# First two heads' scores moved into the projection's tail: one stretch of program order in place of two

## The chip, the cores and the metric

The kernel runs on one core of one Trainium2 chip. The metric is the device time of one execution in microseconds, as the median of several runs. Five engines work side by side, each in the order of its own queue: TensorE (PE, with its weight loads as PEld), VectorE (DVE), ScalarE (ACT), GpSimd (POOL) and SyncE (SP), which issues the transfers.

## The reference

One layer of a diffusion trunk over 1024 latent tokens and 128 context tokens, width 1024. Both token sets are normalised and modulated, then projected once. Group A is a gated MLP that mixes positions inside chunks of 128. Group B is attention with four heads, low-rank queries and keys, and a rotary part of 64. The two are gated, joined and projected out. The part that matters here is attention:

```python
def _block_attention(q_nope, q_ropes, key_sets):
    ...
        for qr, (kn, kr, _) in zip(q_ropes, key_sets):
            logits.append(jnp.einsum('bqhn,bkhn->bhqk', qn, kn)
                          + jnp.einsum('bqhr,bkr->bhqk', qrb, kr))
        s = jnp.concatenate(logits, axis=-1).astype(jnp.float32) * ATTN_SCALE
        p = jax.nn.softmax(s, axis=-1).astype(v_all.dtype)
        return jnp.einsum('bhqk,bkhv->bqhv', p, v_all)
```

Latent tokens read all 1024 latent keys and 256 cached context keys in one softmax. The 128 context tokens of the new request read only themselves. All inputs and outputs are fp32.

## The kernel before

The tokens are nine tiles of 128 (0 to 7 latent, 8 context), in three groups of three tiles. Every fp32 product is made of three (or five) products in a reduced fp32 format: each operand is split into a rounded part and a remainder (names ending in h and l), the rounded part by a cast on ScalarE or GpSimd, the remainder by `lo_of`, a subtraction on VectorE.

The program has these parts: loading, modulating and the v columns; the twelve channel blocks of the wide projection (`channels`); the narrow projection z (448 columns: query rank 256, key rank 128, rope 64), tile by tile in `z_chunk`, with the work that follows from each tile woven between; attention; the output projection.

The weaving is written out by hand. `run((cost, fn))` emits one TensorE step and moves a model clock by its cost; `later(dt, fn)` puts work of the other engines on a list, to be emitted when the model clock has passed its time; `merged` mixes two lists of steps; `need` emits waiting work until a result is marked as made. Inside a block of `tc.manual_schedule` the instructions of PE, ACT, DVE and POOL stay in the order in which they are emitted. An engine's queue is in order, so an instruction that waits holds all behind it.

After the last z tile (t = 8), the projection's tail holds: key transposes (`keys`, kT), the transpose of the last query latents (`cq_transpose(8)`), rotary queries of tiles 6 to 8 (`q_rope`, `q_rope_T`: tiles qr and qrT), and the unrotated queries of group 2 for four heads (`q_nope(2, h)`: qn20 to qn23). The norm of each tile is in `z_stats`: z is copied, squared and summed, and `scales` and `apply` give kvn, scl and nscl. These steps use eight PSUM banks: `pst` (tag t, two banks given out in turn) and `psa` (tag acc, six banks given out in turn). Behind them this block ends, all its pending work is emitted, `psa` is closed, and attention opens `pso` (tag o, one bank) and `pss` (two score tiles s1 of two banks each and one bank s2 for the context part) in its place. A tile that takes an older tile's bank waits until that one has been read.

Attention works through 32 pairs of tile and head. `score_steps(t, h)` gives two latent halves of five 512-wide products (s) and a context part of five 256-wide ones (s2). `softmax` then does, on VectorE, two row maxima (m) and the shift nb; on ScalarE the exponentials (e) with their sums; on VectorE the reciprocal (rs); on GpSimd the scaling of e. Scores run two heads (LEAD) ahead. `value_steps` transposes the probabilities of a pair of heads (pT in `pst`), splits them (ph, pl), multiplies with the values (o) and up-projects (at). `own_steps` is the context tile's attention with itself: scores s8, transposes pT8, product o8 and up-projection at8.

## Time and profile before

| | |
|---|---|
| median of 3 runs | 630.7 us (629.14 to 634.01) |
| the profiled execution | 633.54 us, its span 631.5 us |
| mean granted clock of TensorE | 0.993 |
| busy in the span | PE 97%, PEld 88%, DVE 57%, ACT 42%, POOL 28% |
| chain that ended last | PE 90%, DVE 3%, DMA 3%, ACT 3% |
| z projection, last block starts | 315.2 us |
| projection's tail | 315.4 to 326.8 us |
| first head's scores start | 326.8 us |
| last matmul starts | 623.8 us |

Times inside the execution are counted from the start of the span. The profile's engine rows give the start, the length and the tiles of each instruction, and in brackets how long the engine stood idle before it and which engine ended that. Matmuls overlap, so the distance between two starts says what a matmul costs, and its length is more than that.

### The profile page before, as it was taken

Reading aid. Unit: us, or ns where it says so; the run is one execution under the profiler, and the core shown is the slowest. Engines: PE = TensorE matmul, PEld = TensorE weight load, DVE = VectorE, ACT = ScalarE, POOL = GpSimd, SP = SyncE. Lnnn points to the kernel's source line nnn. Section 1 sums busy time; section 2 is a strip of 40 time slices with the busy share of each in tenths; the row PEclk is TensorE's granted clock in tenths of the full one; section 3 lists DMA queues with packets and bytes.
Section 4 is the critical chain, followed back from the end, with each engine's and each line's share of the span. In section 5 each row is a group of like instructions: output and inputs, shape, how many; then the busy total and the mean of one; then the engine's idle time right before and its main releaser. Section 6 shows DMA issues by size and latency. Waiting matters only on the chain.

```text
span 631.5 us, 9855 instructions
## 1 busy us (share of the span) xinstructions
PE 615.5 (97%) x3733; PEld 558.3 (88%) x3733; DVE 359.0 (57%) x835; ACT 264.2 (42%) x635; POOL 175.2 (28%) x217
## 2 busy tenths in 40 slices
PE   7999999999999999999989999999999999999995
PEld 6677889999999999999977999999999988888884
DVE  2667347037766200356786665776766755487655
ACT  7444774012111011465566556555555543132212
POOL 2525104154433520243353221332222341000001
PEclk8999999999999999999999999999999999999999
DMA  8975100024122430100010000000101112523311
GB/s 324 370 277 169 34 0 2 1 72 178 52 84 95 126 119 1 32 7 1 0 42 2 1 1 0 2 2 34 34 1 34 34 68 84 184 100 134 107 60 66
DMA packets 17118, 46.32 MB, mean 73 GB/s; under 512 B 1952, under 2 KB 6448, under 8 KB 17072
## 3 DMA queue, kind: packets, MB, share of 16 engines
q1 hardware_dynamic: 16928, 45.51, 20.9%
q8 instruction: 29, 0.48, 0.3%
q10 hardware_dynamic: 144, 0.20, 0.1%
q14 instruction: 17, 0.14, 0.1%
HBM read 40.87 MB, written 4.83 MB: 72 GB/s over the span
## 4 chain that ended last, share of the span: by engine, by line
PE 90%; DVE 3%; DMA 3%; ACT 3%; SPq 1%; issue 1%; ACTq 0%
PE tp L670 6%; PE tp L151 6%; PE tp L150 6%; PE tp L152 6%; PE pT L1142 5%; PE w L1389 5%; PE w L1390 5%; PE w L1391 5%; PE o L1166 3%; PE o L1168 3%; PE o L1167 3%; PE s L1097 3%; PE s L1098 3%; PE s L1096 3%; PE s L1095 3%; PE s L1099 3%
## 5 line engine op out<-in xcount | busy, mean ns | idle before, releaser
L104 DVE TENSOR_TENSOR pl<-pT,ph 128x512 fp32r<-128x512 f32 x81 | 55.4, 686 | 48.0 <-ACT ph L1146 47.9
L1086 POOL TENSOR_SCALAR e<-e,rs 128x1280 f32<-128x1280 f32 x32 | 42.8, 1338 | 137.1 <-DVE rs L1085 121.4
L152 PE MATMUL tp<-area,w2l 128*128 128x384 f32 x216 | 72.5, 336 | 0.0
L150 PE MATMUL tp<-area,w2h 128*128 128x384 f32 x216 | 72.5, 336 | 0.0
L151 PE MATMUL tp<-area,w2h 128*128 128x384 f32 x216 | 72.5, 336 | 0.0
L1080 ACT ACTIVATE e<-s,nb,scl 128x256 f32<-128x256 f32 x64 | 56.1, 881 | 36.0 <-DVE nb L1074 35.9
L1146 ACT CAST ph<-pT 128x512 fp32r<-128x512 f32 x80 | 45.4, 589 | 43.2 <-PE pT L1142 40.2
L1142 PE MATMUL pT<-ident,e 128*128 128x128 f32 x320 | 47.9, 272 | 0.6 <-DVE pl L104 0.6
L1166 PE MATMUL o<-ph,vh 128*128 128x256 f32 x160 | 47.8, 299 | 0.0
L104 DVE TENSOR_TENSOR w2l<-w2r,w2h 128x1024 fp32r<-128x1024 f32 x12 | 20.2, 1687 | 43.9 <-POOL w2h L107 43.9
L1168 PE MATMUL o<-ph,vl 128*128 128x256 f32 x160 | 44.9, 281 | 0.0
L1167 PE MATMUL o<-pl,vh 128*128 128x256 f32 x160 | 44.7, 280 | 0.0
L1391 PE MATMUL w<-area,ml 128*128 128x512 f32 (+1 forms) x114 | 43.2, 379 | 0.0
L1142 PEld LDWEIGHTS pT<-ident,e 128*128 128x128 f32 x320 | 37.5, 140 | 4.3 <-DVE pl L104 1.5
L150 PEld LDWEIGHTS tp<-area,w2h 128*128 128x128 f32 x216 | 40.5, 188 | 0.6 <-issue 0.5
L151 PEld LDWEIGHTS tp<-area,w2h 128*128 128x128 f32 x216 | 40.5, 188 | 0.2
L152 PEld LDWEIGHTS tp<-area,w2l 128*128 128x128 f32 x216 | 40.5, 188 | 0.0
L1070 DVE TENSOR_REDUCE m<-s 128x1 f32<-128x1024 f32 x32 | 38.9, 1216 | 1.9 <-PE s L1099 1.9
L1095 PE MATMUL s<-kch,area 128*128 128x512 f32 (+2 forms) x100 | 38.9, 389 | 0.0
L670 PE MATMUL tp<-area,w2h 128*128 128x384 f32 x144 | 37.4, 340 | 0.0
L1098 PE MATMUL s<-krh,area 128*128 128x512 f32 (+2 forms) x100 | 35.4, 354 | 0.0
L1097 PE MATMUL s<-kch,area 128*128 128x512 f32 (+2 forms) x100 | 35.4, 354 | 0.0
(309 smaller groups left out, 1583.6 us busy)
## 6 DMA issues: line engine op xcount, KB each, us to landing
ada<-in_ada_ss SPq DMA_DIRECT2D x16, 512.0 KB, 10.9
w2r<-in_w_t SPq DMA_DIRECT2D x12, 512.0 KB, 4.1
xr<-in_x SPq DMA_DIRECT2D x9, 512.0 KB, 5.0
adag<-in_ada_g SPq DMA_DIRECT2D x8, 512.0 KB
wor<-in_w_o SPq DMA_DIRECT2D x8, 512.0 KB, 3.2
out_y<-y SPq DMA_DIRECT2D x8, 512.0 KB, 2.7
x<-in_x SPq DMA_DIRECT2D x6, 512.0 KB, 8.7
wvr<-in_w_v SPq DMA_DIRECT2D x8, 256.0 KB, 8.2
```

The costliest lines, as they stand in the source:

```text
L104: V.tensor_tensor(lo, src, f32(hi), op=ALU.subtract)
L150: T.matmul(ps, wh, xh, start=j == 0, stop=False)
L151: T.matmul(ps, wh, xl, start=False, stop=False)
L152: T.matmul(ps, wl, xh, start=False, stop=j == n - 1)
L670: T.matmul(tps[i, g][:, :GW], w_[i][:, k, :], x_[k, g], start=k == 0 and j == 0, stop=k == NK - 1 and j == 2)
L1080: S.activation(e[:, sl], src, AF.Exp, bias=nb, scale=scl[:, t : t + 1], accum_out=su[:, i : i + 1])
L1095: T.matmul(ps, qh_, kch[:, sl], start=True, stop=False)
L1142: T.transpose(ps[:, w : w + P], es[t, h][:, c * P : (c + 1) * P], ident)
L1166: T.matmul(o, vh[:, kt, :], ph[:, sl], start=c == 0, stop=False)
L1167: T.matmul(o, vh[:, kt, :], pl[:, sl], start=False, stop=False)
L1168: T.matmul(o, vl[:, kt, :], ph[:, sl], start=False, stop=c == n - 1)
L1391: T.matmul(ps, b, woh[k][:, c0:c1], start=False, stop=k == NK - 1)
```

## The change

Projection and attention become one block of program order. `psa` is closed right behind `cq_transpose(8)`, and `pso` and `pss` are opened there. The scores of the first two heads (tile 0, heads 0 and 1), which stood behind the tail, stand among its steps. The tail's own tiles therefore no longer have `psa`: rotary queries of tiles 6 to 8 and unrotated queries of heads 0 and 2 take `pst`, those of heads 1 and 3 take the one bank of `pso`, and the last tile's keys share one `pst` tile at the end (`keys_last`). The query latents cq are kept per group, those of groups 0 and 1 in an own pool that is closed early, and the probabilities of the first two heads get an own pool (e0).

Of the other engines' work: the last tile's squares and norm are due later, the exponentials' table is loaded 2.6 model units behind the key transposes and not at the end, the values' copies on GpSimd are due earlier, and in `scales` the two VectorE operations zv are emitted together in a step of their own. The context tile's own attention moves back: its scores from the first two heads to the next two, its other steps by one round, and o8 takes a `pst` bank.

```diff
@@ z_stats
-                V.tensor_scalar(v[:, c_], ssz[:, c_], 1.0 / width, EPS, op0=ALU.mult, op1=ALU.add)
+            def mean():
+                V.tensor_scalar(v[:, 0:1], ssz[:, 0:1], 1.0 / 256.0, EPS, op0=ALU.mult, op1=ALU.add)
+                V.tensor_scalar(v[:, 1:2], ssz[:, 1:2], 1.0 / 128.0, EPS, op0=ALU.mult, op1=ALU.add)
...
+            at_ = 4.5 if t == NT - 1 else 0.35
             for i, op in enumerate(steps_):
-                later(0.35 + 0.2 * i, op)
-            later(0.35 + 0.2 * len(steps_), lambda: apply(r))
+                later(at_ + 0.2 * i, op)
+            later(at_ + 0.2 * len(steps_), lambda: apply(r))
...
-        later(0.35, squares)
+        last = t == NT - 1
+        later(2.6 if last else 0.35, squares)
         later(0.9, rope_key)
-        later(1.5, scales)
+        later(4.0 if last else 1.5, scales)
@@ q_nope, q_rope, q_rope_T
-        ps = psa.tile([P, 512], F32, tag="acc", name=f"qn{g}{h}")
+        pool = psa if g < 2 else (pst, pso)[h % 2]
+        ps = pool.tile([P, 512], F32, tag="acc" if g < 2 else "to"[h % 2], name=f"qn{g}{h}")
...
-        ps = psa.tile([P, 512], F32, tag="acc", name=f"qr{t}")
+        ps = (pst if t == NS else psa).tile([P, 512], F32, tag="t" if t == NS else "acc", name=f"qr{t}")
...
-        late = t == NS
+        late = t >= 6
@@ new
+    def keys_last():
+        need(("k", NS))
+        ps = pst.tile([P, 512], F32, tag="t", name="kT8")
+        T.transpose(ps[:, 0:P], kvn[:, NS, :], ident)
+        T.transpose(ps[:, P : 2 * P], krd[:, NS, :, :].rearrange("p a r -> p (a r)"), ident)
+        sl = slice(NS * P, NT * P)
+        for i, (dh, dl) in enumerate(((kch, kcl), (krh, krl))):
+            later(0.3 + 0.3 * i, lambda dh=dh, i=i: S.copy(dh[:, sl], ps[:, i * P : (i + 1) * P]))
+            later(0.7 + 0.3 * i, lambda dh=dh, dl=dl, i=i: lo_of(dl[:, sl], ps[:, i * P : (i + 1) * P], dh[:, sl]))
@@ the projection's tail
-        later(11.0, lambda: pool_copy(cv[0], ctxr[:, 2, :]))
...
-            (0.45, lambda: keys(0, 4, 0)),
-            (0.45, lambda: keys(0, 4, 1)),
-            (0.25, lambda: cq_transpose(8)),
-            (0.45, lambda: keys(4, 4, 0)),
-            (0.45, lambda: keys(4, 4, 1)),
+        later(3.5, lambda: pool_copy(cv[0], ctxr[:, 2, :]))
...
+        for kt, kind in ((0, 0), (0, 1), (4, 0), (4, 1)):
+            run((0.45, lambda: keys(kt, 4, kind)))
+        run((0.25, lambda: cq_transpose(8)))
+        closed(c_pa)
+        closed(c_zc)
+        c_po, pso = opened("pso", bufs=1, space=PSUM)
+        c_ps, pss = opened("pss", bufs=2, space=PSUM)
+        c_e0, e0 = opened("e0", side="left")
+        s2 = pss.tile([P, 2, 256], F32, tag="s2", name="s2", bufs=1)
+        later(ETAB, lambda: S.activation(warm_e, ones[:, 0:1], AF.Exp))
+        sc0, sc1 = score_steps(0, 0), score_steps(0, 1)
+        for s_ in (
             (0.45, lambda: q_rope_T(6)),
+            *sc0,
+            (0.75, lambda: q_rope(8)),
             (0.45, lambda: q_rope_T(7)),
-            (0.75, lambda: q_rope(8)),
+            (1.05, lambda: q_nope(2, 1)),
+            *sc1[:1],
             (1.05, lambda: q_nope(2, 0)),
-            (0.15, lambda: keys(8, 1, 1)),
-            (0.15, lambda: keys(8, 1, 0)),
-            (1.05, lambda: q_nope(2, 1)),
+            *sc1[1:],
+            (1.05, lambda: q_nope(2, 3)),
             (1.05, lambda: q_nope(2, 2)),
             (0.25, lambda: q_rope_T(8)),
-            (1.05, lambda: q_nope(2, 3)),
+            (0.25, keys_last),
@@ own_steps, attention
-            o = cell["o"] = pso.tile([P, 512], F32, tag="o", name="o8")
+            o = cell["o"] = pst.tile([P, 512], F32, tag="t", name="o8")
...
-        first = [s_ for i in range(LEAD) for s_ in score_steps(*heads[i])]
-        merged(first[:4] + own[:1] + first[4:], [])
...
             if c == 0:
-                sc = sc[:3] + own[1:2] + sc[3:5] + own[2:3] + sc[5:] + own[3:]
+                sc = sc[:3] + own[:1] + sc[3:]
+            if c == 1:
+                sc = sc[:2] + own[1:2] + sc[2:4] + own[2:3] + sc[4:] + own[3:]
```

The order on TensorE at the end of the projection's tail, before: the single key transposes of tile 8 (kT81, kT80) between two query projections (one row of six is shown of each), and head 0's scores (s100) behind the last.

```order
L966 MATMUL kT81_3260<-ident_75,krd_2372 128x128
L966 MATMUL kT80_3263<-ident_75,kvn_2371 128x128
L150 MATMUL qn21_3266<-cqh_2359,wfh_2361 128x384
...
L150 MATMUL qn22_3277<-cqh_2359,wfh_2361 128x384
...
L946 MATMUL qrT8_3286<-ident_75,qun8_3244 128x128 x2
L150 MATMUL qn23_3290<-cqh_2359,wfh_2361 128x384
...
L1095 MATMUL s100_3328<-kch_3153,area0_117 128x512
```

And now, in the same place (again one row of each group of products), with s100 and s101 the scores of heads 0 and 1:

```order
L1059 MATMUL s100_3231<-kch_3160,area0_117 128x512
...
L151 MATMUL qn21_3290<-cqh2_2359,wfh_2361 128x384
...
L1059 MATMUL s101_3300<-kch_3160,area0_117 128x512
...
L151 MATMUL qn20_3317<-cqh2_2359,wfh_2361 128x384
...
L151 MATMUL qn23_3350<-cqh2_2359,wfh_2361 128x384
...
L151 MATMUL qn22_3361<-cqh2_2359,wfh_2361 128x384
...
L962 MATMUL qrT8_3370<-ident_75,qun8_3279 128x128 x2
L992 MATMUL kT8_3374<-ident_75,kvn_2374 128x128
...
L1059 MATMUL s102_3393<-kch_3160,area0_117 128x512
```

The keys of tile 8 went from the middle of the queries to their end, two tiles of `pst` behind qn22, and all that follows on TensorE (head 2's scores, s102) stands behind them.

ScalarE in the same stretch before: the casts of the queries (qn) and of the last keys, then the table of the exponentials, then the exponentials (e) of head 0.

```order
L920 COPY qun8_3244<-qr8_3237 128x256
L906 CAST area2_119<-qn20_3249 128x384
L969 CAST krh_3155<-kT81_3260 128x128
L969 CAST kch_3153<-kT80_3263 128x128
L906 CAST area2_119<-qn21_3266 128x384
L906 CAST area2_119<-qn22_3277 128x384
L955 CAST area2_119<-qrT8_3286 64x2x128 x2
L906 CAST area2_119<-qn23_3290 128x384
L1047 ACT_TABLE_LOAD
...
L1080 ACTIVATE e00_3343,su00_3341<-s100_3328,nb00_3340,scl_92 128x1024
```

And now:

```order
L1159 ACT_TABLE_LOAD
...
L936 COPY qun8_3279<-qr8_3272 128x256
...
L1044 ACTIVATE e00_3259,su00_3257<-s100_3231,nb00_3256,scl_92 128x1024
L971 CAST area2_119<-qrT7_3285 64x4x128 x2
L922 CAST area2_119<-qn21_3290 128x384
L922 CAST area2_119<-qn20_3317 128x384
...
L1044 ACTIVATE e01_3341,su01_3339<-s101_3300,nb01_3338,scl_92 128x1024
L922 CAST area2_119<-qn23_3350 128x384
L922 CAST area2_119<-qn22_3361 128x384
L996 CAST kch_3160<-kT8_3374 128x128
```

The exponentials of heads 0 and 1 moved ahead of the casts of four query tiles, and those of head 1 (e01) now stand ahead of the casts of qn23 and qn22.

VectorE from the recovery of the last tile's norm (zr8) on, before: keys' and queries' remainders follow it, and the first row maximum (m00) stands behind all of them.

```order
L848 SCALAR_TENSOR_TENSOR zr8_3189<-zt8_3190,zr8_3189 128x2
L855 SCALAR_TENSOR_TENSOR kvn_2371<-z8_3147,zr8_3189,kvg_123 128x128
...
L104 TENSOR_TENSOR kcl_3154<-kT40_3199,kch_3153 128x512
L104 TENSOR_TENSOR krl_3156<-kT41_3208,krh_3155 128x512
...
L104 TENSOR_TENSOR area2_119<-qn20_3249,area2_119 128x384
...
L104 TENSOR_TENSOR area2_119<-qn21_3266,area2_119 128x384
L104 TENSOR_TENSOR area2_119<-qn22_3277,area2_119 128x384
...
L104 TENSOR_TENSOR area2_119<-qn23_3290,area2_119 128x384
L1070 TENSOR_REDUCE m00_3339<-s100_3328 128x1
```

And now, from the same norm:

```order
L105 TENSOR_TENSOR area2_119<-qn21_3290,area2_119 128x384
...
L859 SCALAR_TENSOR_TENSOR zt8_3245<-zt8_3245,zv8_3242 128x2
L860 SCALAR_TENSOR_TENSOR zr8_3244<-zt8_3245,zr8_3244 128x2
L868 SCALAR_TENSOR_TENSOR kvn_2374<-z8_3154,zr8_3244,kvg_123 128x128
...
L105 TENSOR_TENSOR area2_119<-qn20_3317,area2_119 128x384
L1034 TENSOR_REDUCE m01_3337<-s101_3300 128x1
...
L1038 SCALAR_TENSOR_TENSOR nb01_3338<-m01_3337,nscl_93 128x1
L105 TENSOR_TENSOR area2_119<-qn23_3350,area2_119 128x384
...
L105 TENSOR_TENSOR area2_119<-qn22_3361,area2_119 128x384
```

The norm moved from ahead of the key remainders to behind head 0's softmax, and head 1's maxima and shift stand ahead of the remainders of qn23 and qn22.

## The prediction

> **What bounds the kernel now.** I read the busy shares first, then TensorE's own waits, then the order of time on the four engines from 315 to 348 us, and last the granted clock in stretches. The first part of the page and TensorE's waits of the whole span (us in total, times, longest) stand here.

> ```profile
> PE 615.5 (97%) x3733; PEld 558.3 (88%) x3733; DVE 359.0 (57%) x835; ACT 264.2 (42%) x635; POOL 175.2 (28%) x217
> engine line waited for: us in total, times, longest us
> PE modp L336 <- DMA ada<-in_ada_ss: 1.9, 2, 1.4
> PE warm L460 <- DVE onesr L231: 1.4, 1, 1.4
> PE qrT L946 <- DVE krl L104: 1.2, 1, 1.2
> PE vacc L452 <- DVE area L104: 1.1, 1, 1.1
> PE qr L152 <- DVE cql L104: 1.0, 1, 1.0
> PE pT L1142 <- DVE pl L104: 0.6, 2, 0.4
> ...
> PE at L1329 <- ACT e L1320: 0.4, 1, 0.4
> PE qr L150 <- ACT cqh L893: 0.2, 1, 0.2
> ```

> TensorE sets the time. The change leaves its arithmetic as it is, so the time moves only by TensorE's idle time and its clock. In the stretch that is rewritten the waits are qrT 1.2, qr 1.0 and 0.2, at 0.4 and one pT of 0.4: together 3.2 us. That is all that better order there can win; the other waits lie at the start, before any edit.

> **What the work costs.** TensorE's order of time (start, length, engine, line) gives the length of each piece by the distance of starts.

> ```profile
> 315.38 0.60 PE L966 MATMUL kT<-ident,kvn 128*128 128x128 f32 x4
> 315.82 0.60 PE L966 MATMUL kT<-ident,krd 128*128 128x128 f32 x4
> ...
> 320.63 0.34 PE L150 MATMUL qn<-cqh,wfh 128*128 128x384 f32 x1
> ...
> 321.68 0.27 PE L966 MATMUL kT<-ident,krd 128*128 128x128 f32 x1
> ...
> 326.84 0.39 PE L1095 MATMUL s<-kch,area 128*128 128x512 f32 x1
> ...
> 328.00 0.40 PE L1095 MATMUL s<-kch,area 128*128 128x512 f32 x1
> ...
> 329.15 0.28 PE L1095 MATMUL s<-kch,area 128*128 128x256 f32 x1
> ...
> 329.75 0.40 PE L1095 MATMUL s<-kch,area 128*128 128x512 f32 x1
> ```

> A transpose is 0.11 us, a query projection 1.05, a latent half of a head's scores 1.16, the context part 0.60. By the context part the qr product, six matmuls of the same width, is 0.70. Now ScalarE's order of time, then VectorE's, and two rows of GpSimd's.

> ```profile
> 315.63 0.53 ACT L876 COPY z<-zacc 128x448 f32<-128x448 f32 x1 [0.23 <-PE zacc L988]
> 316.06 0.39 ACT L832 ACTIVATE j<-zacc 128x256 bf16<-128x256 f32 x1
> ...
> 316.83 0.58 ACT L969 CAST kch<-kT 128x512 fp32r<-128x512 f32 x1
> ...
> 324.40 0.48 ACT L906 CAST area<-qn 128x384 fp32r<-128x384 f32 x1 [0.56 <-PE qn L152]
> ...
> 331.26 0.56 ACT L1080 ACTIVATE e<-s,nb,scl 128x256 f32<-128x256 f32 x1 [2.22 <-DVE nb L1074]
> ...
> 332.91 0.19 ACT L1080 ACTIVATION_READ_ACCUMULATOR e<-s,nb,scl 128x1 f32 x1
> ...
> 317.90 0.67 DVE L104 TENSOR_TENSOR kcl<-kT,kch 128x512 fp32r<-128x512 f32 x1
> 318.49 0.22 DVE L846 TENSOR_TENSOR zt<-zr 128x2 f32<-128x2 f32 x1
> ...
> 322.54 2.60 DVE L956 TENSOR_TENSOR area<-qrT,area 64x512 fp32r<-64x512 f32 x4
> 325.38 0.55 DVE L104 TENSOR_TENSOR area<-qn,area 128x384 fp32r<-128x384 f32 x1
> 329.35 1.23 DVE L1070 TENSOR_REDUCE m<-s 128x1 f32<-128x1024 f32 x1 [0.84 <-PE s L1099]
> 330.50 0.41 DVE L1073 TENSOR_REDUCE m<-s 128x1 f32<-128x256 f32 x1
> 330.94 0.22 DVE L1074 SCALAR_TENSOR_TENSOR nb<-m,nscl 128x1 f32<-128x1 f32 x1
> ...
> 339.25 1.17 DVE L1074 SCALAR_TENSOR_TENSOR nb<-m,nscl 128x1 f32<-128x1 f32 x1
> ...
> 339.07 1.34 POOL L1086 TENSOR_SCALAR e<-e,rs 128x1280 f32<-128x1280 f32 x1 [1.40 <-ACT ph L1303]
> ...
> 334.68 1.34 POOL L1086 TENSOR_SCALAR e<-e,rs 128x1280 f32<-128x1280 f32 x1 [8.64 <-DVE rs L1085]
> ```

> One head's softmax is 1.8 us on VectorE (329.35 to 331.16) and 1.84 on ScalarE (331.26 to 333.10), and the second waits for the first. The rows at 339 show VectorE's one-column nb, 0.22 elsewhere, taking 1.17: it ends as GpSimd's scaling of e ends (340.4).

> **The change part by part.** The early arithmetic up to the last z block keeps its order, so I set the new order on the old clock from 315.38, the first key transpose. One thing decides below: pst has two PSUM banks, given out in turn, and the last queries now take these and one of pso instead of the six of psa.

> *First wait: scores of head 0.* 18 transposes for keys and cq and four for qrT6 end at 315.38 + 22 x 0.11 = 317.8. The two-bank score tile lies on a bank that held keys 4 to 7, free when VectorE has made the third key remainder. ScalarE now casts the keys ahead of the squares, so kch is cast at 316.1, done 316.7; three remainders, 0.6 apart and 0.67 long, end at 318.6. TensorE waits 0.8.

> *Second wait: qn23.* Head 0 runs from 318.6 to 321.5 (2 x 1.16 + 0.60). Then qr8 0.70, qrT7 0.44, qn21 1.05, half a head 1.16, qn20 1.05, the rest of head 1 1.76: TensorE is at qn23 at 327.7. It needs the single pso bank back from qn21, whose remainder stands on VectorE behind head 0's softmax. On ScalarE four key casts from 316.1 (0.58 long, 0.1 of each under the next as with z and j: about 0.5), the squares (316.06 to 316.83: 0.8), cqh (0.3) and two casts of qrT6 (0.5) end at 320.2; VectorE's two qrT6 remainders (0.65 each) end at 321.6, nb of head 0 at 323.4. Exponentials to 325.2, two qrT7 casts to 326.3, their remainders to 327.6, five small operations 0.5, qn21's remainder 0.55: 328.7. That is a wait of 1.0. The exponentials' table, loaded early beside this, is hidden by the wait of ScalarE for nb.

> *Third wait: the last tile's keys.* qn23, qn22 (1.05 each) and qrT8 (0.22) bring TensorE to 331.0. kT8 takes the bank of qn22, two pst tiles back. qn22's cast stands on ScalarE behind head 1's exponentials, these wait for nb of head 1, and that stands on VectorE behind the last tile's norm. That norm's first scalar_tensor_tensor meets GpSimd's 1.34 us scaling of head 0 (begun 328.0): held to 329.4. Four operations more, 0.8; qn20's remainder 0.5; softmax 1.8: nb at 332.4. Exponentials to 334.2, the cast of qn23 to 334.7, its remainder and two small operations to 335.5, qn22's remainder to 336.0. That is a wait of 5.0. If VectorE were free as head 1's scores end, nb would be at 329.1 and the bank free at 332.6: a wait of 1.5. The price lies between; 4.7, since every step on the way stands in program order.

> *Fourth wait: transposes of the first probabilities.* The context tile's own attention moves one pair later.

> ```profile
> 342.82 1.16 PE L1329 MATMUL at<-e,wuv 128*128 128x128 f32 x8 [0.44 <-ACT e L1320]
> ...
> 347.59 0.66 PE L1142 MATMUL pT<-ident,e 128*128 128x128 f32 x4 [0.41 <-DVE pl L104]
> ```

> Before, at8 (8 x 0.11 = 0.9) and its own 0.44 of waiting stood between head 3's scores and this pT, which still waited 0.41 for the remainder of the first. Without them the softmax of head 3, cast and remainder are as long, so the wait grows to 1.7 (0.4 if ScalarE and VectorE are early by as much; 2.4 if the context tile's three 512-wide products, 0.23 each, are missed too).

> At nothing I cost the keys of the last tile as one step in place of two (same transposes), the other places of the value copies on GpSimd (which before stood idle for 8.6 us ahead of its first scaling of e), the own pool for two e tiles, and zv in one step. Their cover is TensorE's work or the third wait itself; without it each is under 0.5.

> The waits come to 0.8 + 1.0 + 4.7 + 1.7 = 8.2 in place of 3.2: 5.0 us more.

> *The clock.* The view in stretches (TensorE's busy us, granted clock, DMA):

> ```profile
> 8.40:11.40 3.00, 1.09 (x16) 0.96 1.01 391
> 11.40:18.10 6.70, 6.17 (x30) 0.51 1.03 412
> ...
> 318.00:327.00 9.00, 6.69 (x39) 1.00 0.05 12
> ```

> and one row of TensorE's order of time in the second of these stretches:

> ```profile
> 13.93 2.77 PE L460 MATMUL warm<-ones,ident 128*128 128x128 f32 x12
> ```

> Idle 1.9 of 3.0 us, TensorE was granted half its clock for 6.7 us; idle 2.3 of 9 in pieces of at most 1.2, it kept all of it. A gap of 4.7 lies beyond the first. From 13.93, where the work is dense again, half the clock lasted 4.2 us, which loses 2.1. The bounds are 0 (no drop) and 3.4 (all 6.7 us). I take 2.1.

> [...]

> The sum against the profiled execution (633.54, its span 631.5 and 2.0 around it): 633.54 + 5.0 + 2.1 = 640.6. The median of the runs lies 2.8 below that execution, so the forecast is 637.8.

> **The rivals.**
> *The clock stays whole:* waits alone, 630.7 + 5.0 = 635.7. For it speaks that the only drop that the trace shows came after two gaps with other work between, not after one gap alone.
> *A short bank wait:* VectorE reaches head 1's softmax early, kT8 waits 1.5 to 2.6, the others (3.5 above) half to all, no drop: 3.3 to 6.1 in place of 3.2, so 631 to 633.5. Against it: the norm and four remainders stand ahead in order.
> *Faster:* qn22's bank is back before TensorE needs it, and the early heads let the first probabilities be ready, so that pT and at no longer wait: all 3.2 goes, less the 0.8 of the first wait, 628.3. It decides at nb of head 1: to free the bank by 331.0 it would have to be made 3.6 ahead of that (332.4 against 336.0), at 327.4, ahead of the end of that head's own scores at 327.7. In program order I see no way, unless ScalarE and VectorE run far ahead of their rows.
> *Worse:* the drop lasts all 6.7 us and VectorE is held by GpSimd at two more places (1.2 each): 641 to 643.
> That the change does nothing is excluded: the order of all four engines is another.

> **How the numbers follow.** Forecast (stall and drop) 0.50, 635.5 to 640.5 by itself; clock whole 0.22; short wait 0.15; faster 0.08; worse 0.05. Predicted 637.8. The range, 631.8 to 641.5, leaves out the faster case, most of the worse and some of the short wait. About 1% (6.3 us) is what a measurement tells from no change, so slower means above 637.0. Of the forecast case about two thirds lie there (0.34), of the clock-whole case a fifth (0.04), and all of worse: 0.43. Faster by over 1% would take twice the 3.2 us that there are: 0.03. Within 1%: 0.54.

> **What would show it.** In the new profile TensorE's longest wait in this part should be kT8 for VectorE, 4 to 5 us near 331 to 336, with qn23 about 1 and the first score about 0.8 ahead of it, and pT about 1.7 near 347; qr, qrT8 and at should be gone from the list. Head 1's nb should stand near 332. The granted clock in the 7 us behind the gap should show about half for three to five. If kT8 waits under 2 us, the chain over ScalarE and VectorE was placed too late and the forecast is wrong; if the gap is there and the clock is 1.00, the last 2.1 go.

## The result and the profile after

The changed kernel takes 639.28 us (median of 6 runs, 637.0 to 641.97) against 631.88 us (6 runs, 629.14 to 634.01) for the kernel before, run beside it: 7.4 us more, a ratio of 1.0121 with a 95% interval of 1.008 to 1.0163. That it is slower is clear. The median lies above the bound of 1%, but the interval reaches below it, so a loss of more than 1% is likely and not shown. Its profiled execution took 639.68 us, with a span of 637.9 and a mean granted clock of 0.989; before it was 633.54, 631.5 and 0.993.

Busy time first, then TensorE's waits in the rewritten stretch (314 to 353 us; columns as before).

```profile
PE 616.6 (97%) x3733; PEld 560.0 (88%) x3733; DVE 355.2 (56%) x835; ACT 264.0 (41%) x635; POOL 182.2 (29%) x217
PE kT L992 <- DVE area L105: 4.8, 1, 4.8
PE pT L1200 <- DVE pl L105: 2.0, 1, 2.0
PE qn L151 <- DVE area L105: 1.3, 1, 1.3
PE s L1059 <- DVE kcl L105: 0.5, 1, 0.5
PE pT L1337 <- DVE pl L105: 0.3, 1, 0.3
```

TensorE runs as many instructions as before (3733), at a somewhat lower clock; qr, qrT and at have left the list, and 8.9 us of waits stand where 3.2 stood: 5.7 more. Now TensorE's order of time at the first key transpose, at the two longest waits, and at the end.

```profile
314.30 0.60 PE L982 MATMUL kT<-ident,kvn 128*128 128x128 f32 x4
...
335.49 0.47 PE L992 MATMUL kT<-ident,kvn 128*128 128x128 f32 x1 [4.81 <-DVE area L105]
335.83 0.78 PE L1059 MATMUL s<-kch,area 128*128 128x512 f32 x1
...
340.24 0.41 PE L1059 MATMUL s<-kch,area 128*128 128x256 f32 x1
...
351.50 0.66 PE L1200 MATMUL pT<-ident,e 128*128 128x128 f32 x4 [2.04 <-DVE pl L105]
...
630.18 0.28 PE L1428 MATMUL w<-area,ml 128*128 128x256 f32 x1
```

Two latent halves behind the long wait take 340.24 − 335.83 = 4.41 us instead of 2 × 1.16 = 2.32: 2.1 lost. The view in stretches (TensorE's busy us, granted clock, DMA) shows why: half the clock from the last third of the gap (333.69) until 340.52, when both halves were done and the context part behind them had begun.

```profile
331.00:336.00 5.00, 0.51 (x3) 0.77 0.02 4
336.00:338.00 2.00, 2.00 (x6) 0.50 0.00 0
338.00:340.00 2.00, 2.00 (x6) 0.50 0.00 0
340.00:342.00 2.00, 2.00 (x17) 0.87 0.00 0
```

From the first key transpose to the start of the last matmul, the part that the change touches, before takes 308.40 us (315.38 to 623.78) and after 315.88 (314.30 to 630.18): 7.5 more, against 5.7 + 2.1 = 7.8 from waits and clock. I call this distance the stretch from here on. The profiled execution as a whole grew by only 6.1 us because the part ahead of the stretch, which the change leaves alone, happened to be 1.1 us shorter, and the rest around the span 0.3 (633.54 − 631.5 against 639.68 − 637.9).

What stood on the way to the long wait: ScalarE's order of time, then VectorE's, then a row of GpSimd's.

```profile
331.91 0.56 ACT L1044 ACTIVATE e<-s,nb,scl 128x256 f32<-128x256 f32 x1 [5.55 <-DVE nb L1038]
...
333.65 0.85 ACT L922 CAST area<-qn 128x384 fp32r<-128x384 f32 x2
...
348.34 0.56 ACT L1044 ACTIVATE e<-s,nb,scl 128x256 f32<-128x256 f32 x1 [2.00 <-DVE nb L1038]
...
350.08 1.07 ACT L1204 CAST ph<-pT 128x512 fp32r<-128x512 f32 x2
...
327.49 0.56 DVE L105 TENSOR_TENSOR area<-qn,area 128x384 fp32r<-128x384 f32 x1
327.96 0.83 DVE L858 TENSOR_TENSOR zt<-zr 128x2 f32<-128x2 f32 x1
...
331.66 0.22 DVE L1038 SCALAR_TENSOR_TENSOR nb<-m,nscl 128x1 f32<-128x1 f32 x1
...
334.89 0.54 DVE L105 TENSOR_TENSOR area<-qn,area 128x384 fp32r<-128x384 f32 x1
...
327.45 1.33 POOL L1050 TENSOR_SCALAR e<-e,rs 128x1280 f32<-128x1280 f32 x1 [3.54 <-DVE zr L857]
```

ScalarE stands idle for 5.55 us waiting for nb of head 1, while the casts of qn23 and qn22 stand behind its exponentials; the remainder of qn22 ends at 334.89 + 0.54 = 335.43, and kT8 starts at 335.49. At pT the order is alike, the cast of the first transposed probabilities (ph, 350.08) behind the exponentials of head 3, which waited for their own nb. But there it is no news: in the kernel before that cast stands behind the same exponentials, whose last long one begins at 345.05.

```profile
346.23 1.07 ACT L1146 CAST ph<-pT 128x512 fp32r<-128x512 f32 x2
```

What is new at pT is that TensorE comes to it earlier.

### The profile page after: what moved, and what is told of

Same layout as the page of the kernel before. It is cut to its first block, busy times and chain, and to the rows that moved or that the text cites. A ratio compares the mean times of both kernels' runs of the same rounds, so it can differ in the third digit from the quotient of the medians.

```text
span 637.9 us, 9851 instructions
## 1 busy us (share of the span) xinstructions
PE 616.6 (97%) x3733; PEld 560.0 (88%) x3733; DVE 355.2 (56%) x835; ACT 264.0 (41%) x635; POOL 182.2 (29%) x217
## 4 chain that ended last, share of the span: by engine, by line
PE 89%; DVE 4%; DMA 3%; ACT 2%; SPq 1%; issue 1%; ACTq 0%; DVEq 0%
PE tp L671 6%; PE tp L153 6%; PE tp L151 6%; PE tp L152 6%; PE pT L1200 5%; PE w L1426 5%; PE w L1427 5%; PE w L1428 5%; PE o L1224 3%; PE o L1226 3%; PE s L1059 3%; PE o L1225 3%; PE s L1061 3%; PE s L1060 3%; PE s L1062 3%; PE s L1063 3%
## 5 line engine op out<-in xcount | busy, mean ns | idle before, releaser
L152 PE MATMUL tp<-area,w2h 128*128 128x384 f32 x216 | 72.5, 336 | 0.0
L152 PEld LDWEIGHTS tp<-area,w2h 128*128 128x128 f32 x216 | 40.5, 188 | 0.2
```

Source lines behind the costliest of these rows:

```text
L152: T.matmul(ps, wh, xl, start=False, stop=False)
```

## The experiments

My theory: the waits arise because a cast that frees a PSUM bank is queued behind exponentials whose nb is late, the context tile's moved attention makes the wait at pT, and the long gap then halves the clock. The rivals were the place of the last tile's norm as the cause, a pT wait that is only an echo of the stalls ahead of it, and a clock that drops only behind one long gap. None of these kernels leaves out a part of the computation; the two filled ones add matmuls whose result nobody reads. Each ratio is against the kernel before as run beside it (631.69 us, 22 runs, for the half filled gap, the early norm and the two mended orders; 632.46 us, 16 runs, for the other four).

**Queries ahead of head 1's softmax.** The changed kernel, with head 1's context maximum and shift emitted 2.6 model units later, so that the work on qn23 and qn22 goes first.

```diff
-                later(1.2, cell["start"])
+                later(1.2 + hold[0], cell["start"])
...
-            later(0.7, cell["shift"])
+            later(0.7 + hold[1], cell["shift"])
...
-        sc0, sc1 = score_steps(0, 0), score_steps(0, 1)
+        sc0, sc1 = score_steps(0, 0), score_steps(0, 1, (0.0, 2.6))
```

> The changed kernel, but head 1's context maximum, shift and exponentials are emitted later, so that on ScalarE and VectorE the casts and remainders of qn23 and qn22 stand ahead of them. If the bank of qn22 is what the last tile's keys wait for, kT8's wait falls from 4.8 us to 2 to 2.5, and the clock behind it stays whole; pT, whose cover shrinks, waits 2.5 to 3 in place of 2.0. First key transpose to last matmul: 315.9 in the changed kernel, 311.5 to 312.5 here; time about 4 us under the changed kernel. Rival (the softmax chain of the first heads bounds the stretch, and the bank only shows it): pT's wait grows by all that kT8's loses, and only the clock's 2 us come back.

Measured: 636.09 us (10 runs, 634.33 to 638.16), ratio 1.0057 (1.0036 to 1.0078); the stretch 313.30 us. Two of TensorE's waits, and its stretches behind kT8 and behind pT:

```profile
PE pT L1200 <- DVE pl L105: 2.9, 1, 2.9
PE kT L992 <- DVE area L105: 2.2, 1, 2.2
...
335.00:337.00 2.00, 2.00 (x14) 1.00 0.00 0
...
350.00:353.00 3.00, 3.00 (x13) 0.53 0.00 0
```

The order of two pieces of work on ScalarE and VectorE takes 2.6 us off the kT8 wait, as in the theory, and the clock stays whole there. But head 1's softmax is now late and pushes back those behind it: head 3's first row maximum starts 1.3 us behind its last score product (343.04 behind 341.74), in the changed kernel 0.5 (346.47 behind 345.97). So pT waits 2.9 instead of 2.0, and the clock drops behind that gap instead. I had not foreseen that second drop, so the stretch came out about 1 us above what I expected. By the ratios about half of the change's loss goes (1.21% to 0.57%).

**The gap filled.** The changed kernel, with 17 matmuls on constants into a free score bank ahead of kT8. They keep TensorE busy through most of the wait and change nothing in the data's order.

```diff
+        idle = pss.tile([P, 2, 512], F32, tag="s1", name="idle", bufs=2)
+        for _ in range(17):
+            T.matmul(idle[:, 0, 0:P], ident, ones, start=True, stop=True)
         ps = pst.tile([P, 512], F32, tag="t", name="kT8")
```

> The changed kernel with 17 transposing-size matmuls of constants on TensorE between qrT8 and kT8, into a score bank that is free: about 4.4 us of work in the gap, nothing else moved. If the gap halves the granted clock, this run keeps 1.00 in the 7 us behind it and is about 2 us faster than the changed kernel (313.5 to 314 from first key transpose to last matmul), though TensorE has more to do. If the clock cost nothing, the time is the same or longer.

Measured: 637.93 us (4 runs, 637.0 to 639.0), ratio 1.0087 (1.0059 to 1.0116); the stretch 314.73 us. TensorE's rows at the stretch's start and at kT8, and its stretches behind kT8 and behind pT:

```profile
312.77 0.60 PE L982 MATMUL kT<-ident,kvn 128*128 128x128 f32 x4
...
333.96 0.33 PE L995 MATMUL kT<-ident,kvn 128*128 128x128 f32 x1 [0.99 <-DVE area L105]
...
335.00:337.00 2.00, 2.00 (x12) 1.00 0.00 0
...
347.00:350.00 3.00, 2.36 (x11) 0.62 0.00 0
```

kT8 starts 21.19 us behind the first key transpose, exactly as without the filling (335.49 − 314.30): the wait is set by the other engines, and being busy does not shorten it. The clock, however, is whole behind it. From kT8's start to the context tile's first product TensorE now takes 3.17 us (333.96 to 337.13) instead of 5.48 (335.49 to 340.97). So 2.3 us, the 2.1 of the two halves among them, are the gap's price by way of the clock. In this execution the clock then fell behind the 2.0 us wait of pT, which gave part of it back. The gain is shown by the trace alone: the ratio's interval overlaps that of the changed kernel (1.008 to 1.0163).

**The gap half filled.** The same with 8 matmuls instead of 17, to leave a gap shorter than the changed kernel's 4.8 us: at the start of the kernel before, 1.9 us idle in 3.0 had half the clock behind them (0.51 over 6.7 us).

> The changed kernel with 8 matmuls of constants, about 2.1 us, at the front of the long gap: about 2.7 us of idle time are left in one piece. [...]

Measured: 637.03 us (4 runs, 636.73 to 638.5), ratio 1.0079 (1.0055 to 1.0104); the stretch 315.20 us.

```profile
PE kT L995 <- DVE area L105: 3.0, 1, 3.0
...
331.00:333.00 2.00, 0.00 (x0) 1.00 0.00 0
333.00:335.00 2.00, 1.51 (x7) 0.88 0.00 0
335.00:337.00 2.00, 2.00 (x7) 0.50 0.00 0
337.00:339.00 2.00, 2.00 (x15) 0.77 0.00 0
```

A gap of 3.0 us is enough for half the clock, here for about 3.4 us: (0.12 + 0.50 + 0.23) × 2.00 = 1.7 lost, 1.7 / 0.5 = 3.4 long. The ratio came out no higher than the filled one's, and the intervals of the changed kernel, the filled and the half filled one overlap, so the times don't decide.

**Two gaps for one.** The changed kernel, with qrT8 and the last keys ahead of qn23 and qn22, so that the wait falls into two parts with work between.

```diff
-            (1.05, lambda: q_nope(2, 3)),
-            (1.05, lambda: q_nope(2, 2)),
             (0.25, lambda: q_rope_T(8)),
             (0.25, keys_last),
+            (1.05, lambda: q_nope(2, 3)),
+            (1.05, lambda: q_nope(2, 2)),
```

> The changed kernel with the last rotary queries and the last tile's keys ahead of qn23 and qn22 on TensorE. The two-bank rotation then makes kT8 wait about 2.7 us and qn22 about 3.0: the same idle time in two pieces with about a microsecond of work between. [...]

Measured: 640.4 us (4 runs, 637.52 to 641.56), ratio 1.0119 (1.0082 to 1.0156); the stretch 317.20 us.

```profile
PE kT L992 <- DVE area L105: 2.8, 1, 2.8
...
327.00:331.00 4.00, 1.00 (x7) 0.83 0.00 0
331.00:333.00 2.00, 2.00 (x8) 0.50 0.19 49
333.00:335.00 2.00, 0.38 (x2) 0.50 0.00 0
...
339.00:341.00 2.00, 2.00 (x10) 0.79 0.00 0
```

Neither gap (2.8, then one of 1.7 at qn22) is as long as the changed kernel's 4.8, and the clock was at half from about 330 to 340. So a clock that drops only behind one long gap does not describe this run. Splitting a gap did not save the clock here; it stretched the drop over both parts. This execution has a second drop, behind pT's wait of 2.0 (0.58 from 353 to 356 us), which is part of its long stretch.

**The context tile's steps alone.** The kernel before, with only the context tile's own attention moved as the change moves it (and o8 in `pst`).

```diff
-        merged(first[:4] + own[:1] + first[4:], [])
+        merged(first, [])
...
-                sc = sc[:3] + own[1:2] + sc[3:5] + own[2:3] + sc[5:] + own[3:]
+                sc = sc[:3] + own[:1] + sc[3:]
+            if c == 1:
+                sc = sc[:2] + own[1:2] + sc[2:4] + own[2:3] + sc[4:] + own[3:]
```

> The kernel before with one part of the change alone: the context tile's own scores between heads 2 and 3, its other steps one round later, its product in a pst bank; the projection's tail as before. If the fourth wait comes from this part, pT waits 2 to 3 us in place of 0.4, at's 0.4 goes, and the time is 1.5 to 2.5 us above the kernel before. Rival (the fourth wait is an echo of the stall ahead of it): pT waits 0.5 or less and the time is that of the kernel before.

Measured: 635.29 us (7 runs, 634.29 to 637.95), ratio 1.0059 (1.0034 to 1.0084); the stretch 312.68 us, 4.3 more than before.

```profile
PE pT L1142 <- DVE pl L104: 2.7, 1, 2.7
...
347.00:350.00 3.00, 2.71 (x14) 0.53 0.00 0
```

With no stall ahead of it, pT waits 2.7 instead of 0.4, and the at wait is gone. So the wait at pT is made by this move (o8's new bank is part of it) and is no echo of the stalls. In this execution the clock fell behind it as well: the move alone has both a wait and a drop of its own. Alone it waits longer than within the change (2.0). The trace fits a hold by GpSimd: nb of heads 1 and 2 takes 1.16 and 1.23 us instead of 0.22, each ending as a scaling of e ends (333.65 and 337.56), and head 3's first row maximum starts 1.15 us behind its last score product (341.32 behind 340.17), in the changed kernel 0.5.

**The norm early.** The changed kernel, with the last tile's squares and norm due as in the kernel before.

```diff
-            at_ = 4.5 if t == NT - 1 else 0.35
+            at_ = 0.35
...
-        later(2.6 if last else 0.35, squares)
+        later(0.35, squares)
...
-        later(4.0 if last else 1.5, scales)
+        later(1.5, scales)
```

> The changed kernel with the last tile's squares and norm due as in the kernel before, ahead of the key casts and not behind head 0's softmax. If the norm's place behind head 0's softmax is the cause of the long wait, kT8 waits 2 us or less and the time is 3 us or more under the changed kernel. My theory says that the bank waits for head 1's exponentials in any case: kT8 waits 3 to 3.8 in place of 4.8, and what it gains comes back as a longer wait of the first scores and of qrT6 (about 1 us each); the time stays within 1.5 us of the changed kernel.

Measured: 639.64 us (2 runs, 639.34 and 639.94), ratio 1.0116 (1.0081 to 1.0151); the stretch 317.92 us.

```profile
PE kT L992 <- DVE area L105: 3.2, 1, 3.2
PE pT L1200 <- DVE pl L105: 2.0, 1, 2.0
PE s L1059 <- DVE kcl L105: 2.0, 1, 2.0
```

kT8's wait falls by 1.6 and the first score's grows by 1.5; with 0.8 at qrT, 0.5 at qn and 0.3 at pT8 the sum is 8.8, as it was. The norm's place moves the wait but is not its cause. The stretch is 2.0 longer than the changed kernel's at the same waits. In this execution the clock fell three times: behind the first score's wait (0.76 from 314 to 321 us), behind kT8, and behind pT (0.72 and 0.71 in the two stretches from 350 to 356 us).

**Both orders mended.** The first experiment, and in the second round of values the first two score steps run, and the own transposes stand, ahead of the value steps.

```diff
-            if c == 1:
-                sc = sc[:2] + own[1:2] + sc[2:4] + own[2:3] + sc[4:] + own[3:]
             if not sc:
                 break
+            if c == 1:
+                for s_ in sc[:2]:
+                    run(s_)
+                sc = own[1:2] + sc[2:4] + own[2:3] + sc[4:] + own[3:]
```

> The run with the queries first, and in the round of heads 4 and 5 two pieces of scores and the context tile's transposes ahead of the first probabilities' transposes, to cover the fourth wait. Waits by the order: kT8 2.2, qn23 1.2, pT 1.8 and 0.8, the first score 0.5: no gap over 2.3. First key transpose to last matmul 310.5 to 311.5 in place of 313.3 with the queries first alone, if pT's gap is what drops the clock there; time 1 to 2.5 us under that run and still above the kernel before. Rival (the softmax chain alone sets the pace): 313 or more, since work moved ahead only moves the wait.

Measured: 635.96 us (9 runs, 632.55 to 636.5), ratio 1.0051 (1.003 to 1.0073); the stretch 311.47 us.

```profile
PE kT L992 <- DVE area L105: 2.2, 1, 2.2
PE pT L1200 <- DVE pl L105: 2.1, 2, 1.5
```

The profiled execution has about the waits expected (6.1 in all), no drop in this stretch, and 3.1 us more than before. The 1 to 2.5 us under the first experiment did not come: over all runs the two can't be told apart (1.0051 and 1.0057), and both stay above the kernel before. What remains are waits for a bank to be read (kT8 2.2, qn 1.3, the first score 0.5) on `pst` and `pso`, where the order before had the six banks of `psa`. No run gave the queries more banks, so that two banks are what keeps these waits is argued and not shown.

**The old order mended.** The kernel before, with the casts of the last query latents earlier, the last tile's squares and scales later, and qrT8 behind qn23.

```diff
-        later(0.35, squares)
+        later(1.0 if t == NT - 1 else 0.35, squares)
...
-        later(1.5, scales)
+        later(2.15 if t == NT - 1 else 1.5, scales)
...
-        later(0.4, lambda: S.copy(dh, src))
-        later(0.85, low)
+        later(0.05 if last else 0.4, lambda: S.copy(dh, src))
+        later(0.5 if last else 0.85, low)
...
-            (0.25, lambda: q_rope_T(8)),
             (1.05, lambda: q_nope(2, 3)),
+            (0.25, lambda: q_rope_T(8)),
```

> The kernel before with small edits in the projection's tail alone: the last query latents' cast and remainder, and behind them the last tile's squares, due in another order, and qrT8 behind qn23. If the 2.4 us that TensorE waits in that tail can be had by the order of the evictions, with scores left where they were, qr waits about 0.4 in place of 1.2, qrT8 0.2 in place of 1.2, the last tile's keys about 0.8 where they did not wait: 1.2 us less from first key transpose to last matmul (307.2 against 308.4) and a time 0.1 to 0.3% under the kernel before. Rival: the waits only move on, and the time is the same.

Measured: 630.9 us (12 runs, 629.03 to 632.44), ratio 0.9981 (0.9964 to 0.9999); the stretch 307.30 us, 1.1 less than before.

```profile
PE kT L966 <- DVE kvn L855: 1.1, 1, 1.1
...
PE qrT L946 <- DVE krl L104: 0.2, 1, 0.2
```

The qr waits of 1.0 and 0.2 are gone and qrT's went from 1.2 to 0.2, at the price of 1.1 at kT. This is the one version ahead of the kernel before, by 0.2%, with an interval that just stays below 1. It recovers a third of the 3.2 us of waits within the old order; the change, which had the same waits in view, pays more than twice all of them.

## Why the prediction was right, step by step

The forecast of 637.8 us lies 1.5 below the measured 639.28, inside the range. Set against the kernel before as measured each time, +7.1 was forecast and +7.4 came. That the two lie so close is in part luck: profile against profile the growth is 6.1, and the median moves with drops of the clock that differ from execution to execution. The case named likeliest, a stall and a clock drop, is the one that the trace shows.

- **First wait** (first score): 0.8 placed, 0.5 measured, for the remainder named: the wait's releaser is kcl. It ends at 317.49, which is 318.57 on the old clock (1.08 us later, the distance of the two starts of the stretch); 318.6 was placed. TensorE came at 318.15 and not at 317.8.
- **Second wait** (qn23): 1.0 placed, 1.3 measured. qn21's remainder ends at 328.05, which is 329.1 on the old clock; 328.7 was placed.
- **Third wait** (kT8): 4.7 taken, 4.8 measured. nb of head 1 is ready at 331.88 (333.0 on the old clock, 332.4 placed) and the bank at 335.43 (336.5, 336.0 placed). TensorE too came 0.8 later than placed (335.49 − 4.81 + 1.08 = 331.8 for 331.0), so the difference held, by two delays of about the same size, which is luck in the number and not in the mechanism. Within this chain one detail was wrong: GpSimd's scaling did hold VectorE, but at the norm's TENSOR_TENSOR (0.83 us for two columns) and not at the scalar_tensor_tensor after it.
- **Fourth wait** (pT): 1.7 taken, 2.0 measured. The reason given holds: from the last product of head 3's scores to this pT it is 5.48 us before (342.11 to 347.59) and 5.53 after (345.97 to 351.50), so the chain is as long and only TensorE's cover is gone. The experiment with the context tile's steps alone puts 2.7 on the move by itself, above the upper bound of 2.4; there GpSimd's holds on nb, which the prediction did not place in this chain, come on top.
- **Not in the sum**: a wait of 0.3 at pT8, which comes with the moved steps of the context tile (that experiment has it too, 0.3). The edits costed at nothing show no wait of their own. The waits' sum was 8.2 forecast and 8.9 measured.
- **The clock**: 2.1 taken; 2.1 measured in the two halves (2 × 1.16 us of work took 4.41), 2.3 with kT8 and the context part. Half the clock lasted 6.8 us, 5.0 of them behind the gap (335.49 to 340.52) where 4.2 were taken. That agreement is for this profiled execution. The price of a second drop, behind pT, stands nowhere in the sum, and the trace of the changed kernel has none (348.00 to 350.00 at 1.00), but five of the experiments show it (0.53, 0.53, 0.58, 0.62 and 0.72 over 3 us each). Whether it falls into the changed kernel's longer executions was not seen in a trace. Its runs point that way: the two shortest (637.0 and 637.19 us) had a mean clock of 0.994 and 0.992, the two longest (641.97 and 641.39) 0.989 and 0.987.
- **The median against the profiled execution**: the 2.8 us subtracted were right for the three runs then shown (630.7). With six runs the median before is 631.88, so 1.7 would have been the better term, and 638.9 the forecast.

Of the rivals, "clock whole" falls with the windows at 0.50; "short bank wait" and "faster" with nb at 333.0 on the old clock, 5.6 us behind the 327.4 at which "faster" would have decided; "worse" is right in one point, a drop as long as all 6.7 us (6.8 here), but VectorE was held by GpSimd only once in the chain.

The row from which the prediction took its drop, 1.9 us idle in 3.0, was a good guide: in the experiments half the clock came behind gaps of 3.0, 2.9, 2.7 and 2.0 us too, all shorter than the 4.7 that it priced.

## What to carry to other kernels

Before work is pulled forward to fill a wait, count the buffers that it will need at its new place: with two banks in turn, every tile waits until the one two before it has been read, and the read may stand behind a softmax on another engine (kT8 waited 4.8 us for qn22's). A cast that frees a bank belongs ahead of an operation that itself waits, and moving it is a matter of two numbers (2.6 us of wait here, of which 0.9 came back at pT). A gap on TensorE is to be priced with its clock: in these traces each gap of 2.7 us or more in the rewritten stretch had half the clock behind it, and those of 2.0 to 2.2 some of the time. That cost another 1 to 2 us on top of 2 to 5 us of waiting. It went with where the gap fell in windows of 3.41 us, and their place differed between traces (one begins at 11.19 us in the kernel before and at 12.84 in the changed one).

## What the runs showed of the hardware that was not expected

**The clock halves after short gaps, and not each time.** Gaps with half the clock behind them: 4.8 (after), 3.2 (the norm early), 3.0 (half filled), 2.9 (queries ahead), 2.8 with 1.7 (two gaps), 2.7 (the context tile alone) and 2.0 (pT in the filled, the two-gap and the early-norm kernels, and the first score in the last of these). Gaps with a whole clock: 2.0 at pT in the changed kernel, 2.1 at pT in the half filled one, 2.2 at kT8 in the first experiment and the one with both orders mended. At about 2 us both happen with the same instructions.

```profile
347.35:350.76 3.41, 2.10 (x14) 1.00 0.01 2
344.34:347.75 3.41, 1.39 (x8) 1.00 0.01 2
347.75:351.16 3.41, 3.41 (x16) 0.50 0.00 0
```

In the changed kernel the wait is shared between two windows, and the first of them was idle for 1.3 us; in the filled one it lies in one window, idle for 2.0, and the next window runs at half. In the kernel before and the changed one, cut into windows like these up to the end of the work, half the clock followed those at full clock that were idle for 3.01 us (330.28 to 333.69, after), 1.91 (7.77 to 11.19, before) and 1.53 (9.43 to 12.84, after). It did not follow one that was idle for 1.53 at the end of the work (622.17 to 625.59, before), nor any that was idle for 1.31 or less. That the idle time within a window decides is my reading of these rows; no run was made to test it.

**The same drop makes part of the spread between executions of one kernel.** The stretches at the program's start, the same work in every kernel here, in the changed kernel (first two rows) and in the filled one (last two):

```profile
8.40:11.40 3.00, 1.77 (x24) 1.00 1.02 395
11.40:18.10 6.70, 6.15 (x36) 0.75 1.03 414
```

```profile
8.40:11.40 3.00, 1.91 (x25) 1.00 1.00 377
11.40:18.10 6.70, 6.15 (x52) 1.00 1.03 413
```

With the 0.51 of the kernel before, these clocks of 0.51, 0.75 and 1.00 go with a first key transpose at 315.38, 314.30 and 312.77: the more idle time in the transfers' shadow at 8.40 (1.91, 1.23 and 1.09 of the 3.00 us), the lower the clock and the later everything behind. The first experiment and the two-gap one keep to this order (idle for 2.01 and 1.89 there, clocks of 0.51 and 0.56, first key transpose at 314.98 and 314.82). Among the first three that is up to 2.6 us, as much as many edits are worth, so a span is better compared from the first touched instruction than from zero.

**A small operation on VectorE was held until GpSimd was done.** The two-column TENSOR_TENSOR at 327.96, 0.22 in the kernel before, took 0.83 and ended with GpSimd's scaling of e (327.45 + 1.33 = 328.78). The remainder of qn21 (327.49), which ran beside the same scaling, took its usual 0.56. Why the one was held and the other not, no run shows.
